# One block of p's projection made behind the gate blocks and kept, and the convolution's blocks summed on VectorE

## The chip, the cores and the metric

The kernel runs on one core of a Trainium2 chip. The metric is the device time of one execution in microseconds. TensorE multiplies matrices, VectorE does elementwise work with two operands, ScalarE does activations and copies, GpSimd (POOL) does small work and issues accumulating transfers, and SyncE (SP) issues the loads.

## The reference

One layer of a streaming encoder, for 512 tokens of width 1024, in float32:

```
h = h + 1/2 SwiGLU_1(RMSNorm(h))
z = RMSNorm(h) @ W_in                    # conv value | conv gate | q | k | v | r | low rank
y_conv = silu(LayerNorm(depthwise_conv31(a * sigmoid(b))))          # 512 channels
y_gla  = RMSNorm_per_head(chunked gated linear attention) * silu(r) # 4 heads of 128
h = h + concat([y_conv, y_gla]) @ W_out
h = h + 1/2 SwiGLU_2(RMSNorm(h))
h = h + sigmoid(RMSNorm(h) @ W_g) * (p @ W_p)                       # p: 512 x 256, W_p: 256 x 1024
out = RMSNorm(h)
```

## The kernel before, in words

**Products.** To keep float32 accuracy each operand is split into a rounded high part and a low part (the rest), and a product is three fast passes on TensorE: high by high, low by high, high by low. ScalarE makes the high part (a copy that rounds), VectorE the low part (a subtraction). For some weights the low part is made by ScalarE (times -1) and a transfer of GpSimd's queue that adds the original (`added`, L238). The mean of the LayerNorm is a product with a constant matrix `mean` in full float32, which TensorE runs as two slower passes.

**Layout.** Activations lie transposed: eight tiles `hT` of 128 channels by 512 tokens. The gate r and the values v are made per block of 128 tokens (`tokblock`, L1200). The convolution has four blocks of 128 channels, accumulators `acc[0]` to `acc[3]` (tiles named `cv` in the trace); each takes 31 steps ("taps") on VectorE, and `taps(n)` (L1016) puts n of them into VectorE's order at that place, alternating between two blocks. A step that finds its block finished issues nothing.

**Order.** `Ordered` (L36) fixes the order of TensorE, VectorE and ScalarE to the program's order through the whole stage that the change touches (`in_order(True)`, L996, to `in_order(False)`, L1801). GpSimd's and SyncE's instructions are issued by their own queues, in program order where they are ready.

**The stage of the change.** For t = 0 to 3 (L1365 to L1401) TensorE makes a gate block. Inside block 0 it also makes `outputs(0)` and inside block 1 `outputs(1)`, the attention's outputs, whose squares ScalarE sums at once. Behind block 1 VectorE runs `taps(15)`, then the root of the mean squares (`so`, `rso`; five taps between), ScalarE scales the sixteen head blocks (`y`), and VectorE multiplies each y by its silu(r). Then 16 transposes turn y into four banks `yps`; the products of `mean` with `acc[0]` and `acc[1]` stand before and behind the last four transposes. `gsplit` (L204) rounds each of the four turned heads (tiles `yg`). `first_part(n, ..)` (L1358) starts output block n with the four attention heads, 12 passes; blocks 0, 1, 4, 5, 2, 3 and 6 follow. VectorE meanwhile finishes the last convolution block, adds `acc[2]` and `acc[3]` into `acc23`, and the third mean product, in the middle of block 5, completes the LayerNorm's mean `mub`. From there VectorE, ScalarE and TensorE make the LayerNorm, whose results are the other four operands of the output product.

**The last stage.** p's transposed matrix is loaded behind the output weights (L1418) and split in the second FFN (`split_p`, at the units ("m2", 10) and ("m6", 10)). At the end `inputs(t, e)` (L1698) makes, for token block t and half e of the columns, p's product (`pq`, six passes) and turns h (`pt`, four transposes); `parts_of` (L1712) takes sigmoid, product, sum and squares. The last block but one is `inputs(0, 1)` (L1870).

**Buffers.** `bt` and `bt2` (L90 to L100) take halves of 20 buffers "A"; weights as loaded lie in six buffers "raw"; `bank()` (L127) goes round seven banks of PSUM, `aux()` has the eighth.

The places of the change, with their lines (the last stage of the gate blocks and the start of the output products):

```
1371        elif t == 1:
1372            ps = tokblock(wr, t, {2: lambda: outputs(1)})
1373            taps(15)
...
1402    yps = [bank() for _ in range(4)]
1403    mub = aux()
1404    for t in range(TB):
1405        if t == 3:
1406            pe.matmul(mub, mean, acc[0], start=True, stop=False)
1407        for h in range(4):
1408            pe.transpose(yps[h][:, t * P:(t + 1) * P], ytok[t][:, h * HV:(h + 1) * HV], ident)
1409    pe.matmul(mub, mean, acc[1], start=False, stop=False)
1410    taps(1)
1411    for h in range(4):
1412        mix[4 + h] = gsplit(yps[h], vec("gla_norm", h), "yg")
...
1436    first_part(5, wo[5], {6: lambda: pe.matmul(mub, mean, acc23, start=False, stop=True)})
```

Of the kernel before, what the change touches and what calls it, by code (L numbers as in the profile page):

```python
# [15 lines left out]
P = 128  # L16
# [46 lines left out]
def block_kernel(ctx: ExitStack, tc: tile.TileContext, a: dict, out: bass.AP):  # L63
# [38 lines left out]
    def cvt(dt=F32, s="cv"):  # L102
        return big.tile([P, SEQ], dt, tag="CV", bufs=NCV, name=nm(s))
# [134 lines left out]
    def added(w):  # L238

        h3, l3, r3 = w  # L240
        act.mul(l3, r3, -1.0)
        pool.dma_start(out=l3.bitcast(F32), in_=r3, accum_op=ALU.add)
        return w
# [754 lines left out]
    def pair(c0):  # L998

        return [load(w_in, 0, DC, c0 + i * P, P) for i in range(2)]  # L1000

    glu, acc, conv = [], [cvt() for _ in range(4)], []

    def conv_steps(c):
# [195 lines left out]
    def tokblock(w, t, mid={}):  # L1200

        ps = bank()
        ts = slice(t * P, (t + 1) * P)
        i = 0
        for k in range(DC):
            wh, wl = w[k // 2][:2]
            xh, xl = hg[k]
            for x, y in ((xh, wh), (xl, wh), (xh, wl)):
                if i in mid:
                    mid[i]()  # L1210
                pe.matmul(ps, x[:, ts], y[:, k % 2, :], start=(i == 0), stop=(i == 3 * DC - 1))
                i += 1
        return ps
# [64 lines left out]
    def outputs(t2):  # L1278
        ops.extend([bank(), bank()])
        for t in (2 * t2, 2 * t2 + 1):  # L1280
            for h in range(4):
                pe.matmul(out_of(t, h), sc[h][:, t, :], vt[t][:, h * HV:(h + 1) * HV],
                          start=(t % 2 == 0 and h < 2), stop=False, skip_group_check=True)
        for t in (2 * t2, 2 * t2 + 1):
            for j in range(2):
                for i in range(2):
                    c = 2 * t + i
                    for h in (2 * j, 2 * j + 1) if c else ():
                        d = slice((h % 2) * HK, (h % 2 + 1) * HK)
                        pe.matmul(out_of(t, h)[i * CH:(i + 1) * CH], qdec[j][d, c * CH:(c + 1) * CH],  # L1290
                                  states[j][c][0][d], start=False, stop=(t % 2 == j == 1), skip_group_check=True)
        for t in (2 * t2, 2 * t2 + 1):
            junk = tmp("sq", 2 * SEQ)[:, 0:SEQ]
            for h in range(4):
                act.activation(junk[:, h * HV:(h + 1) * HV], out_of(t, h), AF.Square,
                               accum_out=so[:, 4 * t + h:4 * t + h + 1])
# [7 lines left out]
    for t in range(TB):  # L1304
# [22 lines left out]
        if t == 0:  # L1327
            for j in range(2):
# [4 lines left out]
                act.copy(kd, kp)  # L1333
                kdt.append(kd)

    raw_o = {}

    def oload(n):
# [26 lines left out]
    for t in range(TB):  # L1365
        if t == 0:
            taps(3)
            ps = tokblock(wr, t, {5: lambda: chunk_sums([6]), 12: lambda: outputs(0)})
            chain(range(4, 7))
            oload(4)  # L1370
        elif t == 1:
            ps = tokblock(wr, t, {2: lambda: outputs(1)})
            taps(15)
            by_t = "p (t h) -> p t h"
            so3 = so.rearrange(by_t, h=4)
            dve.tensor_tensor(out=so3, in0=so3, in1=rs2.unsqueeze(2).to_broadcast([P, TB, 4]), op=ALU.mult)
            rso = rsqrt_mean(so, HV * HK, 16, between=lambda: taps(5))
            rso3 = rso.rearrange(by_t, h=4)
            dve.scalar_tensor_tensor(out=rso3, in0=rso3, scalar=HK ** -0.5,
                                     in1=rs.unsqueeze(2).to_broadcast([P, TB, 4]), op0=ALU.mult, op1=ALU.mult)  # L1380
        else:
            ps = tokblock(wr, t)
        r = bt(s="r")
        act.activation(r, ps, AF.Silu, scale=rs[:, t:t + 1])
        rt.append(r)
        if t == 1:
            oload(2)
            wo[4] = [added(w) for w in ohigh(4)]
            ytok = []
            for i in range(TB):  # L1390
                y = bt(s="y")
                for h in range(4):
                    vs = slice(h * HV, (h + 1) * HV)
                    act.activation(y[:, vs], out_of(i, h), AF.Copy, scale=rso[:, 4 * i + h:4 * i + h + 1])
                ytok.append(y)
        if t == 2:
            wo[5] = [added(w) for w in ohigh(5)]
        if t > 0:
            taps((0, 2, 5, 2)[t])
            for i in {1: (0,), 2: (1, 2), 3: (3,)}[t]:  # L1400
                dve.tensor_tensor(out=ytok[i], in0=ytok[i], in1=rt[i], op=ALU.mult)  # L1401
    yps = [bank() for _ in range(4)]
    mub = aux()
    for t in range(TB):
        if t == 3:
            pe.matmul(mub, mean, acc[0], start=True, stop=False)
        for h in range(4):
            pe.transpose(yps[h][:, t * P:(t + 1) * P], ytok[t][:, h * HV:(h + 1) * HV], ident)
    pe.matmul(mub, mean, acc[1], start=False, stop=False)
    taps(1)  # L1410
    for h in range(4):
        mix[4 + h] = gsplit(yps[h], vec("gla_norm", h), "yg")
    wo[2] = added(ohigh(2))
    wo[3] = ohigh(3)
    oload(6)


    p_raw = [bt(s="p") for _ in range(2)]  # L1418
    for k in range(2):
        nc.sync.dma_start(out=p_raw[k], in_=a["pT"][k * P:(k + 1) * P])  # L1420
    first_part(0, wo[0])
    first_part(1, wo[1])
    for steps in list(conv):
        for _ in steps:
            pass
    conv.clear()
    acc23 = bt(s="acc23")
    dve.tensor_tensor(out=acc23, in0=acc[2], in1=acc[3], op=ALU.add)
    low(wo[3])
    ffn2_in = a["ffn2_w_in"]  # L1430
    wf = {i: Left(ffn2_in, 2 * i) for i in range(3)}
# [1 line left out]
    w0.fetch("a11", "a12", "a21", "a22")  # L1433
    w1.fetch("a11", "a12")
    first_part(4, wo[4])
    first_part(5, wo[5], {6: lambda: pe.matmul(mub, mean, acc23, start=False, stop=True)})
    first_part(2, wo[2])
    sqs, lln, yc = [], [], []
    for c in range(4):
# [59 lines left out]
    for k in range(4):  # L1499
# [4 lines left out]
            pe.matmul(ps, wl, mix[k][0], start=False, stop=False)  # L1504
        for n in range(3):
            pe.matmul(half[n][1], rows_of(half[n][0], k)[0], mix[k][1], start=False, stop=(k == 3))
    pT = []

    def split_p(k):
        pT.append(split(p_raw[k], "pT"))  # L1510
# [54 lines left out]
    w1.part("s3")  # L1565
    w2.add_part("a12")
    hooks = sums_hooks(xb, ("t4",), (("m2", 1),))
    hooks.update({("m2", 10): lambda *_: split_p(0), ("m6", 10): lambda *_: split_p(1)})

    w_gate = a["ple_w_gate"]  # L1570
    q11, q21, q12, q22, b11, b21, t2, wproj = ([] for _ in range(8))
# [123 lines left out]
    sse = tmp("sse", 16, bufs=1)  # L1695
    hf, hl = {}, {}

    def inputs(t, e, small=False):  # L1698

        wh, wl = wproj[e][:2]  # L1700
        ts = slice(t * P, (t + 1) * P)
        pq, pt = bank(), aux() if small else bank()
        for k in range(2):
            xh, xl = pT[k]
            pe.matmul(pq, xh[:, ts], wh[:, k, :], start=(k == 0), stop=False)
            pe.matmul(pq, xl[:, ts], wh[:, k, :], start=False, stop=False)
            pe.matmul(pq, xh[:, ts], wl[:, k, :], start=False, stop=(k == 1))
        for c in range(4):
            pe.transpose(pt[:, c * P:(c + 1) * P], hT[4 * e + c][:, ts], ident)
        return pq, pt  # L1710

    def parts_of(t, e, z, pq, pt, c0=0, c1=SEQ, by=act):  # L1712
# [154 lines left out]
    i3 = inputs(3, 0, True)  # L1867
    z3 = plus(w_[1], both[:, 1])
    whole(2, 0, z2, *i2)
    i0 = inputs(0, 1)  # L1870
    times(x_, s4_, b22, last=True, blocks=((0,),))
    whole(3, 0, z3, *i3)
    cols = [slice(0, HALF), slice(HALF, SEQ)]
# [76 lines left out]
```

## Time and profile before

| | |
|---|---|
| median of 3 runs | 926.2 us (925.75 to 926.48) |
| profiled execution | 924.51 us, span 922.8 us |
| TensorE busy | 913.8 us (99%) |
| VectorE busy | 816.5 us (88%) |
| ScalarE busy | 509.3 us (55%) |
| mean granted clock of TensorE | 0.998 |

Times in the profile count from the start of the span. A row of a timeline gives start, duration, engine, line, operation, tiles (output <- inputs), shape and count, and in brackets how long the engine stood idle before it and which engine's instruction ended the wait. All instructions go through a helper, so their line is L46; they are told apart by their tiles. PEld are TensorE's weight loads, which overlap its products. The ends of matmuls are modelled, so the distance between two starts is the better measure of what one takes.

### The profile page before, as it was taken

The numbers are of one execution on the slowest core, as the hardware profiler recorded it, in microseconds if no ns is written. First come the engines' busy times: TensorE is split into PE (matmuls) and PEld (weight loads), VectorE is DVE, ScalarE is ACT, GpSimd is POOL, SyncE is SP. The second block draws the span as 40 slices with busy tenths as digits, with TensorE's granted clock in tenths as the row PEclk, the third lists the DMA queues.
The fourth block names the chain that finished last, engine by engine and source line by source line (L and its number), as shares of the span: only waits on it lengthen the run. The fifth ranks groups of instructions, "written<-read, shape, count | busy, mean of one in ns | idle before, by whom it ended". The sixth has DMA issues, their size and how long they took to land.

```text
span 922.8 us, 12837 instructions
## 1 busy us (share of the span) xinstructions
PE 913.8 (99%) x4952; PEld 780.3 (85%) x4952; DVE 816.5 (88%) x1091; ACT 509.3 (55%) x741; POOL 58.6 (6%) x75
## 2 busy tenths in 40 slices
PE   9999999999999999999999999999999999999996
PEld 8899888888888887788877889888888888888885
DVE  6699989999989776999996779899999999997996
ACT  7755354444454674463565875455445444456883
POOL 0120000000000111001120020000000000000121
PEclk9999999999999999999999999999999999999999
DMA  9534333223334692245562563333224322348463
GB/s 350 184 100 135 113 111 119 90 82 126 114 92 114 164 292 50 72 116 153 137 137 92 137 159 92 114 123 128 85 78 136 114 92 89 100 139 244 91 114 115
DMA packets 36317, 117.58 MB, mean 127 GB/s; under 512 B 4128, under 2 KB 4512, under 8 KB 36256
## 3 DMA queue, kind: packets, MB, share of 16 engines
q1 hardware_dynamic: 29776, 96.83, 31.7%
q0 software_dynamic: 6336, 19.93, 11.8%
q8 instruction: 39, 0.64, 0.3%
q14 instruction: 22, 0.18, 0.1%
q10 hardware_dynamic: 144, 0.00, 0.0%
HBM read 95.77 MB, written 2.10 MB: 106 GB/s over the span
## 4 chain that ended last, share of the span: by engine, by line
PE 99%; DVE 1%; issue 0%; ACT 0%; POOLq 0%; DVEq 0%
PE ps L46 59%; PE pd L46 40%; DVE u L46 0%; DVE rs L46 0%; ACT yc L46 0%; DVE y L46 0%; DVE g L46 0%; DVE s L46 0%; DVE lnsq L46 0%; POOLq L1946 0%; DVE ms L46 0%; DVE sse L46 0%; DVEq L46 0%; POOLq L46 0%
## 5 line engine op out<-in xcount | busy, mean ns | idle before, releaser
L46 DVE TENSOR_TENSOR wl<-wr,wh 128x1024 fp32r<-128x1024 f32 (+2 forms) x159 | 186.0, 1180 | 16.2 <-ACT wh L46 15.9
L46 ACT CAST wh<-wr 128x1024 fp32r<-128x1024 f32 (+2 forms) x177 | 175.3, 1022 | 15.9 <-PE ps L46 9.4
L46 PE MATMUL pd<-hg,wh 128*128 128x512 f32 x576 | 150.0, 391 | 0.0
L46 PE MATMUL ps<-act,wh 128*128 128x512 f32 x448 | 137.9, 389 | 0.0
L46 PEld LDWEIGHTS pd<-hg,wh 128*128 128x128 f32 x576 | 105.9, 188 | 21.1 <-DVE u L46 0.3
L46 PE MATMUL ps<-hg,wh 128*128 128x512 f32 (+1 forms) x448 | 117.0, 345 | 0.0
L46 PEld LDWEIGHTS ps<-act,wh 128*128 128x128 f32 x448 | 84.1, 188 | 17.5
L46 PE MATMUL pd<-t,wh 128*128 128x512 f32 x392 | 95.3, 391 | 0.0
L46 ACT ACTIVATE s<-g 128x512 f32<-128x512 f32 x48 | 30.4, 633 | 117.5 <-DVE g L46 117.5
L46 ACT COPY sq<-pd 128x1024 f32<-128x1024 f32 x45 | 45.8, 1017 | 86.7 <-PE pd L46 52.4
L46 PEld LDWEIGHTS ps<-hg,wh 128*128 128x128 f32 x448 | 78.1, 190 | 10.7 <-issue 0.6
L46 PE MATMUL ps<-act,wl 128*128 128x512 f32 x224 | 87.1, 389 | 0.0
L46 PEld LDWEIGHTS pd<-t,wh 128*128 128x128 f32 x392 | 71.4, 188 | 13.4
L46 PE MATMUL pd<-hg,wl 128*128 128x256 f32 (+1 forms) x544 | 81.5, 289 | 0.0
L46 PEld LDWEIGHTS pd<-hg,wl 128*128 128x128 f32 x544 | 73.9, 191 | 5.0
L46 PE MATMUL ps<-hg,wl 128*128 128x512 f32 (+1 forms) x224 | 77.0, 344 | 0.0
L46 ACT CAST wh<-sm 128x1024 fp32r<-128x1024 f32 x42 | 44.1, 1051 | 55.2 <-DVE sm L46 50.1
L46 DVE TENSOR_TENSOR wl<-sm,wh 128x1024 fp32r<-128x1024 f32 x42 | 51.1, 1220 | 4.9 <-ACT wh L46 4.9
L46 DVE TENSOR_TENSOR sq<-pd,sq 128x1024 f32<-128x1024 f32 x45 | 54.8, 1219 | 0.4 <-PE pd L46 0.4
L46 PE MATMUL ps<-wh,hg 128*128 128x512 f32 x176 | 54.7, 392 | 0.0
L46 PE MATMUL pd<-t,wl 128*128 128x256 f32 x392 | 52.4, 283 | 0.0
L46 PEld LDWEIGHTS pd<-t,wl 128*128 128x128 f32 x392 | 50.6, 191 | 1.5
(308 smaller groups left out, 1626.4 us busy)
## 6 DMA issues: line engine op xcount, KB each, us to landing
wr<-in_ffn_w_in SPq DMA_DIRECT2D x84, 512.0 KB, 3.6
wr<-in_ffn_w_out SPq DMA_DIRECT2D x32, 512.0 KB, 3.6
wl<-wr POOLq DMA_DIRECT2D x20, 512.0 KB, 5.4
wr<-in_ffn_w_out SPq DMA_DIRECT2D x16, 384.0 KB, 3.3
wr<-in_w_blocks SPq DMA_DIRECT2D x12, 512.0 KB, 4.9
wr<-in_w_rows SPq DMA_DIRECT2D x8, 512.0 KB, 3.8
wr<-in_w_out SPq DMA_DIRECT2D x8, 512.0 KB, 4.9
wq<-in_ple_w_gate SPq DMA_DIRECT2D x8, 512.0 KB, 4.3
```

The costliest lines, as they stand in the source:

```text
L46: inst = call(*args, **kwargs)
```

## The change

- `early_parts()` is new. It rounds the first 128 columns of p's transpose (`early_p`) on ScalarE, makes the low part on VectorE, and makes the parts of the second half of W_p's columns (`early_w`) by ScalarE and a transfer of GpSimd. It is called behind gate block 1, ahead of `taps(15)`. The two loads are issued ahead of the output weights.
- The six passes of p's product for token block 0 and column half 1 go into a bank `pq`: two ahead of the last four transposes of y, four behind them, in place of the first two mean products. ScalarE copies the bank to `kept_pq` behind the four `gsplit`. At the end `inputs(0, 1)` shrinks to the four transposes, and `parts_of` reads `kept_pq`.
- VectorE sums the convolution's blocks into `acc012`: `acc[0] + acc[1]` at t = 3, `acc[2]` behind the transposes, `acc[3]` at the end in place of `acc23`; the mean is one product, at the place of the third. `taps(2)` at t = 3 becomes `taps(1)`.
- Output block 0 is written out with its passes in another order: the high parts of a head are used before the low parts.
- The load of p moves from behind the output weights to the second FFN, unit ("m7", 9).

```diff
@@ -998,6 +998,14 @@
     def pair(c0):
 
         return [load(w_in, 0, DC, c0 + i * P, P) for i in range(2)]
+
+    def projected(pq, t, w, x, ks=range(2)):
+
+        ts = slice(t * P, (t + 1) * P)
+        for k in ks:
+            (xh, xl), (wh, wl) = x[k][:2], (v[:, k, :] for v in w)
+            for i, (y, v) in enumerate(((xh, wh), (xl, wh), (xh, wl))):
+                pe.matmul(pq, y[:, ts], v, start=(k == i == 0), stop=(k == 1 and i == 2))
 
     glu, acc, conv = [], [cvt() for _ in range(4)], []
 
@@ -1333,6 +1341,23 @@
                 act.copy(kd, kp)
                 kdt.append(kd)
 
+    early_w = raw(2, SEQ)
+    nc.sync.dma_start(out=early_w, in_=a["ple_w_proj"][0].rearrange("(k p) c -> p k c", p=P)[:, :, SEQ:])
+    early_p = tmp("u2", bufs=1)[:, 0:2 * P].rearrange("p (k c) -> p k c", k=2)
+    nc.sync.dma_start(out=early_p, in_=a["pT"].rearrange("(k p) c -> p k c", p=P)[:, :, 0:P])
+    kept_pq, kept_p = bt(s="pq"), bt(F32R, s="px")
+    early_x, early_wh = [], []
+
+    def early_parts():
+        hi, lo = (kept_p[:, i * 2 * P:(i + 1) * 2 * P].rearrange("p (k c) -> p k c", k=2) for i in range(2))
+        act.copy(hi, early_p)
+        dve.tensor_tensor(out=lo, in0=early_p, in1=hi.bitcast(F32), op=ALU.subtract)
+        early_x[:] = [(hi[:, k], lo[:, k]) for k in range(2)]
+        wh, wl = (wp.tile([P, 1024], F32R, tag="sm", bufs=2, name=nm("sm")).rearrange("p (k c) -> p k c", k=2)
+                  for _ in range(2))
+        act.copy(wh, early_w)
+        early_wh[:] = added((wh, wl, early_w))[:2]
+
     raw_o = {}
 
     def oload(n):
@@ -1370,6 +1395,7 @@
             oload(4)
         elif t == 1:
             ps = tokblock(wr, t, {2: lambda: outputs(1)})
+            early_parts()
             taps(15)
             by_t = "p (t h) -> p t h"
             so3 = so.rearrange(by_t, h=4)
@@ -1395,37 +1421,45 @@
                 ytok.append(y)
         if t == 2:
             wo[5] = [added(w) for w in ohigh(5)]
+        if t == 3:
+            acc012 = bt(s="acc012")
+            dve.tensor_tensor(out=acc012, in0=acc[0], in1=acc[1], op=ALU.add)
         if t > 0:
-            taps((0, 2, 5, 2)[t])
+            taps((0, 2, 5, 1)[t])
             for i in {1: (0,), 2: (1, 2), 3: (3,)}[t]:
                 dve.tensor_tensor(out=ytok[i], in0=ytok[i], in1=rt[i], op=ALU.mult)
     yps = [bank() for _ in range(4)]
-    mub = aux()
+    pq = bank()
     for t in range(TB):
         if t == 3:
-            pe.matmul(mub, mean, acc[0], start=True, stop=False)
+            for x in (0, 1):
+                pe.matmul(pq, early_x[0][x], early_wh[0][:, 0, :], start=(x == 0), stop=False)
         for h in range(4):
             pe.transpose(yps[h][:, t * P:(t + 1) * P], ytok[t][:, h * HV:(h + 1) * HV], ident)
-    pe.matmul(mub, mean, acc[1], start=False, stop=False)
+    pe.matmul(pq, early_x[0][0], early_wh[1][:, 0, :], start=False, stop=False)
+    projected(pq, 0, early_wh, early_x, (1,))
+    dve.tensor_tensor(out=acc012, in0=acc012, in1=acc[2], op=ALU.add)
     taps(1)
     for h in range(4):
         mix[4 + h] = gsplit(yps[h], vec("gla_norm", h), "yg")
+    act.copy(kept_pq, pq)
     wo[2] = added(ohigh(2))
     wo[3] = ohigh(3)
     oload(6)
 
 
-    p_raw = [bt(s="p") for _ in range(2)]
-    for k in range(2):
-        nc.sync.dma_start(out=p_raw[k], in_=a["pT"][k * P:(k + 1) * P])
-    first_part(0, wo[0])
+    ps = bank()
+    half[0] = (wo[0], ps)
+    todo = ((4, 0), (4, 1), (5, 0), (5, 1), (4, 2), (6, 0), (6, 1), (5, 2), (7, 0), (7, 1), (6, 2), (7, 2))
+    for n, (k, i) in enumerate(todo):
+        (wh, wl), (xh, xl) = rows_of(wo[0], k), mix[k]
+        pe.matmul(ps, (wh, wl, wh)[i], (xh, xh, xl)[i], start=(n == 0), stop=False)
     first_part(1, wo[1])
     for steps in list(conv):
         for _ in steps:
             pass
     conv.clear()
-    acc23 = bt(s="acc23")
-    dve.tensor_tensor(out=acc23, in0=acc[2], in1=acc[3], op=ALU.add)
+    dve.tensor_tensor(out=acc012, in0=acc012, in1=acc[3], op=ALU.add)
     low(wo[3])
     ffn2_in = a["ffn2_w_in"]
     wf = {i: Left(ffn2_in, 2 * i) for i in range(3)}
@@ -1433,7 +1467,8 @@
     w0.fetch("a11", "a12", "a21", "a22")
     w1.fetch("a11", "a12")
     first_part(4, wo[4])
-    first_part(5, wo[5], {6: lambda: pe.matmul(mub, mean, acc23, start=False, stop=True)})
+    mub = aux()
+    first_part(5, wo[5], {6: lambda: pe.matmul(mub, mean, acc012, start=True, stop=True)})
     first_part(2, wo[2])
     sqs, lln, yc = [], [], []
     for c in range(4):
@@ -1504,7 +1539,12 @@
             pe.matmul(ps, wl, mix[k][0], start=False, stop=False)
         for n in range(3):
             pe.matmul(half[n][1], rows_of(half[n][0], k)[0], mix[k][1], start=False, stop=(k == 3))
-    pT = []
+    pT, p_raw = [], []
+
+    def load_p():
+        for k in range(2):
+            p_raw.append(bt(s="p"))
+            nc.sync.dma_start(out=p_raw[k], in_=a["pT"][k * P:(k + 1) * P])
 
     def split_p(k):
         pT.append(split(p_raw[k], "pT"))
@@ -1565,7 +1605,7 @@
     w1.part("s3")
     w2.add_part("a12")
     hooks = sums_hooks(xb, ("t4",), (("m2", 1),))
-    hooks.update({("m2", 10): lambda *_: split_p(0), ("m6", 10): lambda *_: split_p(1)})
+    hooks.update({("m7", 9): lambda *_: load_p(), ("m2", 10): lambda *_: split_p(0), ("m6", 10): lambda *_: split_p(1)})
 
     w_gate = a["ple_w_gate"]
     q11, q21, q12, q22, b11, b21, t2, wproj = ([] for _ in range(8))
@@ -1695,18 +1735,15 @@
     sse = tmp("sse", 16, bufs=1)
     hf, hl = {}, {}
 
+    def turned(pt, t, e):
+        for c in range(4):
+            pe.transpose(pt[:, c * P:(c + 1) * P], hT[4 * e + c][:, t * P:(t + 1) * P], ident)
+
     def inputs(t, e, small=False):
 
-        wh, wl = wproj[e][:2]
-        ts = slice(t * P, (t + 1) * P)
         pq, pt = bank(), aux() if small else bank()
-        for k in range(2):
-            xh, xl = pT[k]
-            pe.matmul(pq, xh[:, ts], wh[:, k, :], start=(k == 0), stop=False)
-            pe.matmul(pq, xl[:, ts], wh[:, k, :], start=False, stop=False)
-            pe.matmul(pq, xh[:, ts], wl[:, k, :], start=False, stop=(k == 1))
-        for c in range(4):
-            pe.transpose(pt[:, c * P:(c + 1) * P], hT[4 * e + c][:, ts], ident)
+        projected(pq, t, wproj[e][:2], pT)
+        turned(pt, t, e)
         return pq, pt
 
     def parts_of(t, e, z, pq, pt, c0=0, c1=SEQ, by=act):
@@ -1867,7 +1904,9 @@
     i3 = inputs(3, 0, True)
     z3 = plus(w_[1], both[:, 1])
     whole(2, 0, z2, *i2)
-    i0 = inputs(0, 1)
+    pt0 = bank()
+    turned(pt0, 0, 1)
+    i0 = kept_pq, pt0
     times(x_, s4_, b22, last=True, blocks=((0,),))
     whole(3, 0, z3, *i3)
     cols = [slice(0, HALF), slice(HALF, SEQ)]
```

## The prediction

> **What bounds the kernel now.** I read the page first: the shares of busy time, then the chain that ended last.
>
> ```profile
> PE 913.8 (99%) x4952; PEld 780.3 (85%) x4952; DVE 816.5 (88%) x1091; ACT 509.3 (55%) x741; POOL 58.6 (6%) x75
> ...
> PE 99%; DVE 1%; issue 0%; ACT 0%; POOLq 0%; DVEq 0%
> ```
>
> TensorE has hardly a gap: time is won by taking work off it, and lost by any wait put in front of it. So I read next, engine by engine, the timeline of the stage that the change touches: the four gate blocks (to 471.3 us) and the output projection behind them. VectorE first:
>
> ```profile
> 448.82 1.38 DVE L46 SCALAR_TENSOR_TENSOR st<-st,decay,ps 128x128 f32<-128x128 f32 x5
> 450.11 0.73 DVE L46 SCALAR_TENSOR_TENSOR cv<-en,col,cv 128x488 f32<-128x488 f32 x1
> ...
> 459.81 0.18 DVE L46 TENSOR_TENSOR so<-so,rs 128x16 f32<-128x16 f32 x1
> ...
> 469.79 1.29 DVE L46 TENSOR_TENSOR y<-y,r 128x512 f32<-128x512 f32 x2
> ...
> 472.22 0.69 DVE L46 TENSOR_TENSOR y<-y,r 128x512 f32<-128x512 f32 x1 [0.50 <-ACT r L46]
> ```
>
> The states end at 450.1, `taps(15)` starts at once and ends at 459.8, and the means of the attention outputs (`so`) follow without a gap. VectorE is full here. ScalarE, in its own order:
>
> ```profile
> 457.41 0.25 ACT L46 ACTIVATION_READ_ACCUMULATOR sq<-ps 128x1 f32 x1
> 460.62 0.69 ACT L46 ACTIVATE r<-ps,rs 128x512 f32<-128x512 f32 x1 [2.96 <-PE ps L46]
> ...
> 464.71 4.24 ACT L46 ACTIVATE y<-ps,rs 128x128 f32<-128x128 f32 x16 [1.32 <-DVE rs L46]
> ...
> 471.50 0.69 ACT L46 ACTIVATE r<-ps,rs 128x512 f32<-128x512 f32 x1
> ```
>
> The squares of `outputs(1)` end at 457.66. The sixteen scalings `y` start when VectorE has their factors (464.71), and with the last gate `r` (471.50) ScalarE has run without a gap since then. So the last `y` product (472.22) is tied to VectorE's time at `so`. TensorE:
>
> ```profile
> 471.30 1.47 PE L46 MATMUL ps<-ident,y 128*128 128x128 f32 x12
> 472.61 1.02 PE L46 MATMUL ps<-cv,mean 128*128 128x512 f32 x2
> 473.47 0.60 PE L46 MATMUL ps<-ident,y 128*128 128x128 f32 x4
> 473.91 1.02 PE L46 MATMUL ps<-cv,mean 128*128 128x512 f32 x2
> 474.52 0.64 PE L46 MATMUL ps<-yg,wh 128*128 128x512 f32 x1
> ...
> 480.49 4.25 PE L46 MATMUL ps<-yg,wa 128*128 128x512 f32 x18
> 484.58 1.02 PE L46 MATMUL ps<-acc,mean 128*128 128x512 f32 x2
> ```
>
> The transposes of `y` follow the gate blocks with no slack worth naming: y of blocks 1 and 2 is ready at 471.08, the transposes begin at 471.30. The mean products stand where TensorE would wait for the last `y`.
>
> **The change part by part.** Times are those of the trace of before.
>
> *Mean products.* One takes 0.86 us of TensorE (472.61 to 473.47). Two go: -1.72.
>
> *The block of p's product.* Six wide products at 0.227 us each (18 in 484.58 - 480.49 = 4.09) come in here, +1.36, two ahead of the last four transposes and four behind them. The reordering of the first output block lets TensorE start on the rounded halves; between 474.52 + 0.25 (end of the mean) and 480.49, 24 products should take 5.45 and took 5.72, so about 0.3 us of waits for rounding goes. Taken alone, this stage would save about 0.5 us.
>
> *`early_parts()`: where the time is lost.* It stands behind gate block 1 and ahead of `taps(15)`. Its first instruction, ScalarE's copy of p's block, is queued behind the squares of `outputs(1)`, that is at 457.66. Its second is VectorE's subtraction, which needs that copy and in VectorE's program order stands where the taps now start, at 450.11. Both engines' orders are fixed by the kernel here, so VectorE stands from 450.11 with the fifteen taps, the `so` chain and everything else behind it. The nearest rows for the copies:
>
> ```profile
> L46 ACT CAST wh<-wr 128x1024 fp32r<-128x1024 f32 x159 | 161.5, 1046 | 15.9 <-PE ps L46 9.4 <-DVE wr L46 4.5 <-DMA wr<-in_first_w 1.7
> ...
> L46 ACT CAST hg<-xg 128x256 fp32r<-128x256 f32 x8 | 2.6, 404 | 0.0
> ```
>
> 457.66 + 0.40 = 458.06, and about 0.4 for the subtraction (a 512-wide product takes 0.69 at 472.22, so between half of it and all) gives 458.5; neighbours overlap by about 0.09 (448.82 + 1.38 against 450.11), so the taps start at 458.4: 8.3 us late. Bounds: 7.5 if the copy could start with the last square, 8.7 if it has a start cost like a hand-over. ScalarE's two further instructions (1.05 us each, the copies of 128x1024) fit in its idle 2.96 us before `r`; the accumulating transfer is issued by GpSimd near 460 and is past its queue before the power for `so`, which now comes at 468.5.
>
> Who waits: `so` moves from 459.81 to 468.1, the factors and the sixteen `y` from 464.71 to 473.0, the last `r` from 471.50 to 479.8, the last `y` product from 472.22 to 480.5, ending 481.2. TensorE ends the gate blocks at 471.3 as before (nothing there needs VectorE) and then stands, but for the transposes that come one block at a time.
>
> *To the mean.* Last transposes at 481.35 instead of 473.47; 0.45 for them, 0.91 for the four products, and 42 products (the blocks 0, 1, 4 and half of 5) at 0.227, 9.53: TensorE is at the mean at 492.25. VectorE:
>
> ```profile
> 474.50 2.73 DVE L46 SCALAR_TENSOR_TENSOR yg<-ps,col,yg 128x512 fp32r<-128x512 f32 x4 [0.94 <-ACT yg L46]
> 477.14 6.22 DVE L46 SCALAR_TENSOR_TENSOR cv<-en,col,cv 128x504 f32<-128x504 f32 x8
> 483.39 0.69 DVE L46 TENSOR_TENSOR acc<-cv,cv 128x512 f32<-128x512 f32 x1
> ```
>
> Its roundings start 1.03 behind the last transposes (474.50 - 473.47), so at 482.4, take 2.64, and then come nine taps instead of eight (`taps(2)` became `taps(1)`, and of the two steps before, one was the empty end of a finished block) at 0.78 each, 7.03, and the last sum, 0.69: 492.75. The first two sums fit where TensorE or VectorE waits: one stands in the tap's place before the 0.50 us wait for `r`, the other before the 0.94 us wait for `yg`. So TensorE waits another 0.5 us for the one mean product left and starts it at 492.8, 8.2 us later than 484.58. What follows (LayerNorm, rest of the projection, second FFN) hangs on this and is full again: all of it moves by 8.2.
>
> *The clock.* TensorE has never stood that long in this trace, except at its ends:
>
> ```profile
> 0.84 4.03 PE L46 MATMUL ps<-const-float32-0.0 128*128 128x128 f32 x18 [0.84 <-PEq L1940]
> ...
> 914.90:919.00 4.10, 0.00 (x0) 0.00 (x0) 3.26 (x15) 2.47 (x4) 0.54 (x1) 1.00 0.33 128
> 919.00:920.00 1.00, 0.00 (x0) 0.00 (x0) 0.06 (x1) 0.03 (x1) 0.00 (x0) 0.67 0.10 41
> ```
>
> The eighteen first passes take 0.22 us each where a 128-wide pass later takes 0.11 (twelve transposes in 1.31), for 4.0 us; and 4.4 us after TensorE has gone idle (no busy time from 914.9 on) the granted clock falls to half (0.67 over that slice is half from 919.34). In the changed kernel the stand is from 471.5 to 478.9 with 0.44 us of transposes at 475. I take it that the clock falls. Then 4.0 us from the last transposes on run at half rate and lose 2.0, of which 0.5 is hidden in the wait for the mean: +1.5. Bounds: 0 (the transposes keep it up) and 2.5 (the wake is later or nothing is hidden).
>
> [...]
>
> *The end.* The six products leave the last stage. There they are worth the same 1.36, but TensorE isn't alone:
>
> ```profile
> 910.22 0.67 ACT L46 ACTIVATE s<-ps,rs 128x512 f32<-128x512 f32 x1
> ```
>
> This sigmoid follows the scaling before it on ScalarE without a gap, so it can't move with TensorE, and on VectorE
>
> ```profile
> 913.09 0.42 DVE L46 TENSOR_TENSOR s<-s,ps 128x256 f32<-128x256 f32 x1 [0.68 <-PE ps L46]
> ...
> 915.61 0.41 DVE L46 TENSOR_TENSOR s<-s,ps 128x256 f32<-128x256 f32 x1
> ```
>
> only the 0.68 us wait at 913.09 can go; from there to the last block VectorE runs through. I take -0.7; bounds 0 and -1.36.
>
> *Costed at nothing.* The copy that keeps p's block is one more 128x512 pass of ScalarE, which falls in its idle time before the LayerNorm's squares, and costs 0.63 where that is gone:
>
> ```profile
> 486.36 0.63 ACT L46 ACTIVATE acc<-cv 128x512 f32<-128x512 f32 x1 [7.32 <-DVE cv L46]
> ```
>  The two early loads enter SP's queue ahead of eight loads of the output weights, which wait for buffers anyway and each get the next one; POOL's queue has one more transfer. p's own load moves to the second FFN, behind weight loads fetched seven units ahead: if it waits for a buffer it holds them, 0 to 2 us. The kept block holds a buffer to the end: 0 to 1.
>
> **Sum:** 8.2 + 1.5 - 0.7 = +9.0 on the profiled execution's 924.5 us (span 922.8), which lies 1.7 below the median of 926.2; so 935.2 for the median.
>
> **The rivals.**
> 1. *The clock stays up* because the transposes break the stand: 8.2 - 0.7 = +7.5, 933.7. For it: the only stand seen to halve the clock was unbroken for 4.4 us, and here the pieces are about 3.5 us.
> 2. *The subtraction doesn't hold VectorE* (no slowdown). One mechanism: p's copy runs before the squares. It decides if the copy is done by 450.1. Then the stage saves 0.5, but the sum of the four blocks ends at about 484.5, so the mean starts where it did, and only the end's 0.7 is left: 925.5, within 0.2%. Against: ScalarE's program order.
> 3. *A queue or buffer wait on top*: SP held by p's load, or a late buffer near the end: +2 on the forecast, 937.2.
>
> **How the numbers follow.** Forecast (stall and slow clock) 0.55, rival 1 0.27, rival 2 0.08, rival 3 0.08, rest 0.02 (faster). About 0.2% (1.9 us) is what a measurement of this kernel can tell from no change. Slower 0.90, same 0.08, faster 0.02. The range reaches from rival 1 less a spread of 1 us (bounds of copy and end) to rival 3: 932.6 to 937.3.
>
> **What would show it.** VectorE idle some 8 us near 450 to 458, released by ScalarE's 128x256 copy; the sixteen `y` at 473; TensorE idle in pieces between 471.5 and 481; the mean product at 493 to 495, released by VectorE; granted clock below 1 in the 5 us behind 478; the last stage shorter by less than 1.4. Wrong if VectorE's taps run through at 450.

## The result, and the profile after

The changed kernel takes 933.93 us (median of four runs, 933.12 to 934.93), the kernel before 925.98 beside it: a ratio of 1.0088, 95% interval 1.0076 to 1.0100. It is 8.0 us slower; 935.2 us were forecast. The profiled execution took 933.21 us with a span of 931.2; that of before took 924.51 with 922.8, so the two traces differ by 8.4 in span.

The page after, its line of busy times and the first line of its chain:

```profile
PE 914.9 (98%) x4948; PEld 781.1 (84%) x4948; DVE 818.5 (88%) x1094; ACT 512.1 (55%) x745; POOL 59.6 (6%) x76
...
PE 94%; issue 2%; DVE 2%; DMA 1%; POOL 1%; ACT 0%; POOLq 0%; DVEq 0%; ACTq 0%
```

TensorE has four instructions fewer and still carries the kernel, but its share of the chain falls from 99 to 94%: other engines now decide for some of the time. VectorE's timeline in the changed stage:

```profile
457.94 0.42 DVE L46 TENSOR_TENSOR px<-u,px 128x256 fp32r<-128x256 f32 x1 [7.79 <-ACT px L46]
458.28 0.72 DVE L46 SCALAR_TENSOR_TENSOR cv<-en,col,cv 128x488 f32<-128x488 f32 x1
...
467.98 0.17 DVE L46 TENSOR_TENSOR so<-so,rs 128x16 f32<-128x16 f32 x1
...
480.38 0.69 DVE L46 TENSOR_TENSOR y<-y,r 128x512 f32<-128x512 f32 x1 [0.54 <-ACT r L46]
...
485.12 7.00 DVE L46 SCALAR_TENSOR_TENSOR cv<-en,col,cv 128x503 f32<-128x503 f32 x9
492.15 0.69 DVE L46 TENSOR_TENSOR r<-r,cv 128x512 f32<-128x512 f32 x1
```

Here the time is lost. The subtraction (`px<-u,px`) stands 7.79 us and its releaser is ScalarE's copy; the first tap starts at 458.28 where it started at 450.11, the means `so` at 467.98 instead of 459.81, the last `y` product at 480.38 instead of 472.22: 8.17, 8.17 and 8.16 us late. ScalarE shows why the copy is late:

```profile
457.36 0.25 ACT L46 ACTIVATION_READ_ACCUMULATOR sq<-ps 128x1 f32 x1
457.45 0.45 ACT L46 CAST px<-u 128x256 fp32r<-128x256 f32 x1
...
472.88 1.14 ACT L46 ACTIVATE r<-ps,rs 128x128 f32<-128x128 f32 x4 [9.54 <-DVE rs L46]
```

The copy starts with the last square's result being read out, and ScalarE itself then waits 9.54 us for the `y` scalings (1.32 before; the first lands in a buffer that the trace calls `r`), for factors that VectorE makes late. TensorE, behind both:

```profile
474.90 0.64 PE L46 MATMUL ps<-ident,r 128*128 128x128 f32 x3 [3.49 <-ACT y L46]
476.91 0.48 PE L46 MATMUL ps<-ident,r 128*128 128x128 f32 x1 [1.37 <-ACT y L46]
478.69 1.97 PE L46 MATMUL ps<-ident,y 128*128 128x128 f32 x8 [1.30 <-DVE y L46]
...
488.67 4.24 PE L46 MATMUL ps<-yg,wa 128*128 128x512 f32 x18
492.90 1.12 PE L46 MATMUL ps<-r,mean 128*128 128x512 f32 x2
```

It stands 3.49, 1.37 and 1.30 us in front of the transposes and starts the mean at 492.90 (484.58 before, +8.32; the x2 are the two passes of the one mean product). Its weight load there shows what it waited for last:

```profile
492.90 0.30 PEld L46 LDWEIGHTS ps<-r,mean 128*128 128x128 f32 x2 [0.41 <-DVE r L46]
```

It was VectorE's last sum. In the last stage there is a wait that nothing in the forecast spoke of, TensorE's for a transfer that GpSimd issues (it adds the rounded-off rest of a weight block by DMA):

```profile
891.41 0.50 PE L46 MATMUL ps<-wl,s 128*128 128x512 f32 x1 [0.59 <-DMA wl<-wq]
```

And the end, VectorE's last block sums (before 913.09, with a wait of 0.68, and 915.61):

```profile
921.61 0.41 DVE L46 TENSOR_TENSOR s<-s,ps 128x256 f32<-128x256 f32 x1
...
924.14 0.41 DVE L46 TENSOR_TENSOR s<-s,ps 128x256 f32<-128x256 f32 x1
```

The 0.68 has gone; the last block is 8.53 late.

### The profile page after: what moved, and what is told of

The parts are those of the page before. It is cut to its first block, busy times and chain, and to the rows that moved or that the text cites. A ratio compares the mean times of both kernels' runs of the same rounds, so it can differ in the third digit from the quotient of the medians.

```text
span 931.2 us, 12847 instructions
## 1 busy us (share of the span) xinstructions
PE 914.9 (98%) x4948; PEld 781.1 (84%) x4948; DVE 818.5 (88%) x1094; ACT 512.1 (55%) x745; POOL 59.6 (6%) x76
## 4 chain that ended last, share of the span: by engine, by line
PE 94%; issue 2%; DVE 2%; DMA 1%; POOL 1%; ACT 0%; POOLq 0%; DVEq 0%; ACTq 0%
PE ps L46 55%; PE pd L46 40%; DMA wl<-wq 1%; POOL rs L46 0%; DVE cv L46 0%; DVE rs L46 0%; DVE y L46 0%; DVE s L46 0%; ACT wa L46 0%; POOL wa L46 0%; DVE g L46 0%; DVE u L46 0%; ACT yc L46 0%; ACT y L46 0%; DVE yc L46 0%
```

## The experiments

The theory: VectorE's subtraction, put in program order ahead of fifteen taps and behind a copy that ScalarE can make only after other work, holds VectorE for 7.8 us, and everything else is small. The rival: the added products, buffers and queue entries cost the time, and the wait only takes over idle time. The experiments ran in three groups (`e1_late_low` to `e4_keep_busy`, `e5_spin_aux` to `e8_before_order`, `e9_changed_again` to `e12_late_low_again`), each on one chip and beside its own runs of the kernel before. Times are medians; ratios are to the kernel before of the same group, with 95% intervals. Between groups only the ratios are compared, or the traces. Code is shown in part; `...` marks what is left out.

**1. The subtraction moved, nothing else** (`e1_late_low`, and again as `e12_late_low_again` beside the changed kernel).

```diff
...
     def early_parts():
...
         act.copy(hi, early_p)
-        dve.tensor_tensor(out=lo, in0=early_p, in1=hi.bitcast(F32), op=ALU.subtract)
+        early_lo[:] = [lambda: dve.tensor_tensor(out=lo, in0=early_p, in1=hi.bitcast(F32), op=ALU.subtract)]
...
         if t == 3:
             dve.tensor_tensor(out=acc012, in0=acc[0], in1=acc[1], op=ALU.add)
+            early_lo[0]()
```

> The changed kernel with one move: VectorE's 128x256 subtraction for p's block leaves its place ahead of taps(15) and stands at t == 3, behind the sum of acc0 and acc1. All the work of the change stays. Theory (the subtraction holds VectorE behind ScalarE's late copy, and everything after it slides): the taps start near 450 us instead of 458.3, the LayerNorm's mean starts at 484.6 +- 0.5 instead of 492.90, TensorE's clock stays at 1.00 through 474 to 484, and the total is 0.7 us below the kernel before (the tail's gain), or up to 1 us above that if the wait for a transfer at 891 us stays: 925.2 to 926.3 us. Rival (the lengthening is the cost of the added products, buffers or queue order, and the wait at the subtraction only takes over idle time that would come later): the mean still starts past 490 and the total stays above 931 us.

Measured: 925.21 us against 925.51, ratio 1.000 (0.999 to 1.001). The whole slowdown is gone. VectorE, and TensorE at the mean and in the last stage:

```profile
450.13 0.72 DVE L46 SCALAR_TENSOR_TENSOR cv<-en,col,cv 128x488 f32<-128x488 f32 x1
...
471.61 0.41 DVE L46 TENSOR_TENSOR px<-u,px 128x256 fp32r<-128x256 f32 x1
```

```profile
484.53 1.12 PE L46 MATMUL ps<-r,mean 128*128 128x512 f32 x2 [0.30 <-DVE r L46]
...
883.12 0.50 PE L46 MATMUL ps<-wl,s 128*128 128x512 f32 x1 [0.75 <-DMA wl<-wq]
```

The same subtraction costs no wait at 471.61; the mean starts where it did before (484.58). The wait for the transfer is still there, so it does not come from the stall. Repeated in one group with the changed kernel:

> The changed kernel itself, unaltered, beside the three below on the same chip, since its four runs and those of e5_spin_aux stood beside different runs of the kernel before. 7.8 to 8.4 us over the kernel before, some 933.3 to 934.

> The kernel of e1_late_low again, beside the changed kernel on the same chip: the price of the subtraction's place, taken directly. Theory: 8.3 to 8.9 us under e9_changed_again, 0 to 0.7 us under the kernel before. Rival (part of the first experiment's gain came from another place): 7.5 us or less.

Measured: changed kernel 934.1 (ratio 1.0089, 1.0075 to 1.0103), with the subtraction moved 925.13 (ratio 0.9996, 0.9987 to 1.0005). The place of one 0.42 us instruction is worth 9.0 us, a little over the expected 8.3 to 8.9; the rival of 7.5 or less falls.

**2. A smaller dose of the same wait** (`e2_early_copy`). ScalarE's copy moves ahead of the squares of `outputs(1)`, the subtraction stays.

```diff
...
     def early_parts():
...
-        act.copy(hi, early_p)
         dve.tensor_tensor(out=lo, in0=early_p, in1=hi.bitcast(F32), op=ALU.subtract)
...
         elif t == 1:
+            act.copy(hi, early_p)
             ps = tokblock(wr, t, {2: lambda: outputs(1)})
             early_parts()
```

> The changed kernel with only ScalarE's 128x256 copy of p's block moved ahead, to behind r[0], in front of the squares of the outputs that held it up; the subtraction keeps its place ahead of taps(15). A smaller dose of the same wait. Theory (VectorE stands from 450.1 until the copy has ended): the copy ends near 453.7, the wait is 3.6 us instead of 7.8, the mean starts at 488.2 +- 0.7, the clock stays at 1.00 or drops for less than 2 us, and the total lies 3 to 4.5 us over the kernel before (929 to 930.5). Rival (the place of VectorE's wait does not matter, the added work does): no change from the changed kernel, 933 to 934.5 us.

Measured: 929.92 (ratio 1.0051, 1.0035 to 1.0067), 4.4 over the kernel before. VectorE:

```profile
454.47 0.43 DVE L46 TENSOR_TENSOR px<-u,px 128x256 fp32r<-128x256 f32 x1 [3.45 <-ACT px L46]
454.81 0.72 DVE L46 SCALAR_TENSOR_TENSOR cv<-en,col,cv 128x488 f32<-128x488 f32 x1
```

The taps are 4.7 us late (454.81 against 450.11) and the total is up by 4.4; in the changed kernel they are 8.2 late and the total is up by 8.0 to 8.4. The time follows the dose, roughly: the profiled execution is the slowest of the four (930.43, the others up to 929.95). TensorE's mean,

```profile
489.82 1.12 PE L46 MATMUL ps<-r,mean 128*128 128x512 f32 x2 [0.31 <-DVE r L46]
```

came 0.9 later than the end of the band I gave (488.2 with 0.7 on either side). I had put the copy's end at 453.7; VectorE could go on only at 454.5 and reached the taps at 454.8, 4.7 late instead of 3.6. And a second wait was added, for GpSimd's root of the mean squares:

```profile
468.98 0.18 DVE L46 TENSOR_TENSOR rs<-rs 128x16 f32<-128x16 f32 x1 [0.84 <-POOL rs L46]
```

In the kernel before this wait is 0.21.

**3. The wait alone, put into the kernel before** (`e3_wait_alone`; the loaded block, its copy and the difference are not used by anything).

```diff
...
             ps = tokblock(wr, t, {2: lambda: outputs(1)})
...
+            act.copy(hi, early_p)
+            dve.tensor_tensor(out=lo, in0=early_p, in1=hi.bitcast(F32), op=ALU.subtract)
             taps(15)
```

> The kernel before with the wait alone: the early load of p's block, ScalarE's 128x256 copy and VectorE's subtraction are put ahead of taps(15) as in the changed kernel, their result is not used, and nothing else of the change is made: the mean keeps its three products, p's product is made where it was. Theory (the wait is the whole cost): VectorE is idle for 7.8 us at the subtraction, the mean over acc2 + acc3 comes 8 to 8.7 us later, and the total is 8 to 9.3 us over the kernel before: 934 to 935.3 us, that is 0.7 us over the changed kernel, since the tail's gain is absent. Rival (the wait is harmless by itself): within 1 us of the kernel before.

Measured: 934.89 (ratio 1.0102, 1.0086 to 1.0118), 9.4 over the kernel before, 0.1 above the band. One copy and one subtraction in the wrong place make the old kernel as slow as the changed one:

```profile
457.90 0.42 DVE L46 TENSOR_TENSOR px<-u,px 128x256 fp32r<-128x256 f32 x1 [7.79 <-ACT px L46]
```

**4. The clock.** The forecast priced TensorE's slower clock at 1.5 us. To keep it up, extra products fill the gaps in which TensorE stood.

```diff
     for t in range(TB):
+        for _ in range(14 if t < 2 else 0):
+            pe.matmul(pq, early_x[0][0], early_wh[0][:, 0, :], start=True, stop=True)
         if t == 3:
```

> The changed kernel with 14 more 128x512 products into the bank of p's product, half of them ahead of the transposes of block 0 and half of them ahead of those of block 1, written over by the real product later: TensorE has work where it stood idle, about 3.3 us for each seven at full clock or 6.6 for fourteen ahead of either block. Theory (the halved clock at 476 to 482 us costs nothing, because TensorE waits for VectorE's sum at the mean anyway): the clock reads 1.00 throughout 470 to 490, the mean still starts at 492.9 +- 0.3 and the total is that of the changed kernel within 0.4 us. Rival (the halved clock is on the path and costs 1.5 us, as forecast): the total falls by 1 to 2 us, to 932 to 933 us.

This run (`e4_keep_busy`) has 14 products ahead of each of the two blocks, so 28 where its expectation speaks of 14 (and at 0.227 us each seven products take 1.6 us, not the 3.3 it gives). It missed: 939.16 us (1.0153, 1.0137 to 1.0169). The products write the bank of p's product, and that bank was not free:

```profile
477.41 6.17 PE L46 MATMUL ps<-sm,px 128*128 128x512 f32 x14 [5.77 <-ACT y L46]
483.42 0.60 PE L46 MATMUL ps<-ident,r 128*128 128x128 f32 x4
483.78 3.45 PE L46 MATMUL ps<-sm,px 128*128 128x512 f32 x14
```

They waited for ScalarE's reading of `y`, as the transposes did, ran largely at half rate and pushed the rest back. It says nothing on the clock's price. The next one (`e5_spin_aux`) writes a bank that nothing uses then; its extra products are used by nothing:

```diff
-    pq = bank()
+    pq, spin = bank(), aux()
     for t in range(TB):
+        for _ in range((14, 5, 4, 0)[t]):
+            pe.matmul(spin, early_x[0][0], early_wh[0][:, 0, :], start=True, stop=True)
```

> The changed kernel with 23 more 128x512 products of p's block into a PSUM bank that nothing else uses at that time (14 ahead of the transposes of block 0, 5 ahead of block 1, 4 ahead of block 2; their result is not used), so that TensorE has work in the gaps of 3.49, 1.37 and 1.30 us in which it stood. At 0.23 us each they fill 3.2, 1.1 and 0.9 us. Theory (the halved clock at 476 to 482 us costs nothing at the mean, since TensorE still waits 0.41 us there for VectorE's last sum): the clock reads 1.00 throughout 470 to 490, the mean still starts at 492.9 +- 0.3, TensorE's wait for the sum grows, and the total is that of the changed kernel within 0.5 us: 933.4 to 934.4. Rival (the halved clock is on the path and costs 1.5 us, as forecast): 932 to 932.8 us.

Measured: 932.3 us (ratio 1.0076, 1.0064 to 1.0089), the rival's band, 1.6 below the changed kernel's first median. But the two medians stand beside different runs of the kernel before (925.3 and 925.98), and the trace gives the rival less. TensorE with the extra products:

```profile
471.04 3.33 PE L46 MATMUL ps<-sm,px 128*128 128x512 f32 x14
...
492.47 1.13 PE L46 MATMUL ps<-r,mean 128*128 128x512 f32 x2 [0.34 <-DVE r L46]
```

The mean comes 0.43 earlier than in the changed kernel, and VectorE's first tap was already 0.20 earlier in that execution (458.08 against 458.28), so the clock's price at the mean is 0.2 in this pair of traces. The rest of this trace's gain comes later: the wait for the transfer (0.59 after) does not occur in it. Two causes were mixed, so both had to be varied on one chip. The last stage's order (next experiment) takes the transfer's wait away; with it, once without and once with the extra products:

> The changed kernel with the last stage's ScalarE order of e6_late_low_order. Theory (its wait of 0.59 us, and 1.01 at the weight load, for the late transfer at 891 us is real and the order takes it away): 0.8 to 1.2 us under e9_changed_again. Rival (that wait was one execution's accident): within 0.3 us of it.

> The kernel of e5_spin_aux with the same ScalarE order, to price the halved clock without the late transfer beside it: against e10_changed_order only the 23 extra products differ. Theory (most of the clock's loss lies inside the wait for VectorE's sum, and what is left is the 0.2 us by which the slow transposes delay VectorE's scalings): 0.2 to 0.5 us faster than e10_changed_order. Rival (the full price forecast): 1.2 to 1.6 us faster.

Measured: the changed kernel 934.1, with the order (`e10_changed_order`) 933.11, with order and products (`e11_spin_order`) 932.2. So the order is worth 1.0, as the transfer's theory said, and the extra products 0.9, between the 0.2 to 0.5 and the 1.2 to 1.6. Both steps are small for this measurement: the intervals of `e9_changed_again` (1.0075 to 1.0103), `e10_changed_order` (1.0067 to 1.0092) and `e11_spin_order` (1.0060 to 1.0085) overlap, each with the next. The traces bear out the first step (experiment 5). What the clock did in each profiled execution shows in the windows 470 to 490 us (after the window and its length stand the busy times of PE, PEld, DVE, ACT and POOL, then the granted clock, the DMA share and GB/s). First the changed kernel:

```profile
470.00:490.00 20.00, 13.84 (x59) 11.01 (x58) 18.74 (x33) 13.21 (x30) 4.48 (x4) 0.83 0.42 98
```

The changed kernel again (`e9_changed_again`):

```profile
470.00:490.00 20.00, 14.10 (x56) 11.07 (x55) 18.77 (x33) 13.21 (x30) 5.06 (x4) 0.74 0.37 92
```

With the order (`e10_changed_order`):

```profile
470.00:490.00 20.00, 13.85 (x58) 10.93 (x57) 18.77 (x32) 13.20 (x30) 4.73 (x4) 0.83 0.39 95
```

With order and products (`e11_spin_order`):

```profile
470.00:490.00 20.00, 18.32 (x81) 14.51 (x80) 18.16 (x32) 13.20 (x30) 5.18 (x4) 0.91 0.35 87
```

With the products alone (`e5_spin_aux`):

```profile
470.00:490.00 20.00, 18.04 (x85) 13.83 (x84) 18.87 (x33) 13.23 (x30) 4.28 (x4) 1.00 0.43 102
```

In the changed kernel's trace the clock reads 0.50 throughout 476 to 482. A mean of 0.83 over 20 us is 6.8 us at half rate, 0.74 is 10.4, 0.91 is 3.6. What this costs up to the mean shows in the time from the first tap to the mean:

| execution | granted clock, 470 to 490 | first tap to mean | us |
|---|---|---|---|
| changed kernel | 0.83 | 458.28 to 492.90 | 34.62 |
| `e9_changed_again` | 0.74 | 458.87 to 493.89 | 35.02 |
| `e10_changed_order` | 0.83 | 458.54 to 493.39 | 34.85 |
| `e11_spin_order` | 0.91 | 459.00 to 494.26 | 35.26 |
| `e5_spin_aux` | 1.00 | 458.08 to 492.47 | 34.39 |

The kernel before, `e1_late_low`, `e12_late_low_again`, `e6_late_low_order`, `e7_tail_made_again` and `e8_before_order`, all at 1.00, take 34.40 to 34.47. In `e10_changed_order` VectorE's last sum had ended at 493.09 (492.40 + 0.69) and TensorE came to the mean later, without a wait, so there the slow stretch before it was on the path:

```profile
493.39 1.02 PE L46 MATMUL ps<-r,mean 128*128 128x512 f32 x2
```

So the slow clock costs 0.2 to 0.6 at the mean in three executions of the changed kernel without extra products (against `e5_spin_aux`), depending on where the slow time falls. In `e11_spin_order` the clock fell in spite of the products, for half as long, and the products themselves, at half rate, then stood in the way (the five from 477.72 took 2.48 us, 1.41 in `e5_spin_aux`); its profiled execution is the slowest of its five (933.66, the others 932.12 to 932.41). So the price stays open between 0.2 (trace) and 0.9 (medians); the 1.5 of the forecast is outside.

**5. The late transfer, and the tail.** In the last stage ScalarE is held to cast, negate, cast, negate:

```diff
+    act.on, act.last = True, None
     b3 = [added(later_high(t)) for t in t3]
+    act.on = False
```

> The kernel with VectorE's late subtraction (the first experiment), and one more edit in the last stage: ScalarE is held to cast, negate, cast, negate for the two weight blocks of which GpSimd then adds the rest by DMA, where it went cast, cast, negate, negate. The first of the two transfers can then be issued 0.95 us earlier (near 876.2 instead of 877.12). Theory (the 0.75 us that TensorE waits at 883.1 us for this transfer ate the tail's gain): the wait goes and the total falls by 0.5 to 0.9 us against the first experiment, to 924.3 to 924.7, 0.8 to 1.2 us below the kernel before. Rival (the two transfers share the DMA engines, so that an earlier start gains little, or another wait follows): within 0.3 us of the first experiment, 924.9 to 925.5.

Measured, on the kernel with the subtraction moved (`e6_late_low_order`): 923.85 us against 925.3, ratio 0.9983 (0.9974 to 0.9992). This version is 1.5 us below the kernel before, and 0.45 below the band that its theory gave. GpSimd's issues of the two transfers in the timeline, first in the kernel before:

```profile
877.02 0.86 POOL L46 DMA_DIRECT2D wl<-wq  x1 [14.44 <-ACT wl L46]
878.11 0.86 POOL L46 DMA_DIRECT2D wl<-wq  x1 [0.23 <-DVE s L46]
```

In the changed kernel:

```profile
885.60 1.75 POOL L46 DMA_DIRECT2D wl<-wq  x2 [14.46 <-ACT wl L46]
```

With the new order (`e6_late_low_order`):

```profile
876.53 0.86 POOL L46 DMA_DIRECT2D wl<-wq  x1 [13.51 <-ACT wl L46]
878.28 0.86 POOL L46 DMA_DIRECT2D wl<-wq  x1 [0.89 <-DVE n L46]
```

Before, the second issue stood 0.23 us for a VectorE result, and the two were 1.09 us apart; after, they follow each other at once, and the first lands 5.8 us after its issue instead of 4.6. With the new order they are 1.75 apart and TensorE doesn't wait in any of the five profiled executions that have it. The first landed 5.8 to 6.3 us after its issue, with a wait on TensorE, in five executions with issues at once (changed kernel twice, `e1_late_low`, `e2_early_copy`, `e12_late_low_again`), but without a wait in two others (`e4_keep_busy`, `e5_spin_aux`): it is an event that comes often, not always, and what decides it is open. Why the second issue no longer waits for VectorE is open: the change gives other buffers to the last stage's tiles, and no run varied that alone. The control, the new order in the kernel before (`e8_before_order`):

> The kernel before with the ScalarE order of e6_late_low_order alone, as its control: what this edit is worth without the change. Theory: TensorE waits only 0.20 us for these transfers in the kernel before, so at most 0.2 us: 925.2 to 925.6. Rival (the transfers' times vary from execution to execution and the order is worth as much here): 0.5 to 0.9 us faster than before.

Measured: 924.82 (ratio 0.9995, 0.9986 to 1.0004), 0.5 below the kernel before and 1.0 above `e6_late_low_order`. That is below the theory's band and at the edge of the rival's; its interval holds 1, so medians don't settle it. The trace does for its own execution: from the mean to VectorE's last block sum it takes 431.01 us, the kernel before 431.03. The last run makes the tail's six products again (`e7_tail_made_again`; the kept copy is made and not used):

```diff
-    pt0 = bank()
-    turned(pt0, 0, 1)
-    i0 = kept_pq, pt0
+    i0 = inputs(0, 1)
```

> The kernel of e6_late_low_order with the last stage's p product of block 0 made again by its six products, as in the kernel before; the kept copy is still made and not used. It prices the tail's part of the change by itself. Theory (VectorE's waits bound the end, so the six products' 1.37 us are worth 0.7): 0.5 to 0.9 us slower than e6_late_low_order, the last block of VectorE 0.7 us later. Rivals: TensorE bounds the end (1.2 to 1.4 us slower), or the products are hidden there (within 0.2 us).

Measured: 924.82 (ratio 0.9997, 0.9988 to 1.0006), 0.97 above `e6_late_low_order`, a little over the theory's 0.5 to 0.9 and below the 1.2 of the rival. VectorE's next-to-last block in the timeline of `e7_tail_made_again`:

```profile
913.69 0.42 DVE L46 TENSOR_TENSOR s<-s,ps 128x256 f32<-128x256 f32 x1 [0.69 <-PE ps L46]
```

And of `e6_late_low_order`:

```profile
912.70 0.41 DVE L46 TENSOR_TENSOR s<-s,ps 128x256 f32<-128x256 f32 x1
```

The wait of 0.69 us is back with the products. Of the 0.99 between the two rows 0.27 stood between the executions already at the first tap (450.69 against 450.42), which leaves 0.72. This is the tail's price, and it bears out that VectorE, not TensorE (1.37), bounds it.

The time from the mean's start to VectorE's last block sum puts the tail and the transfer side by side, free of what happened before the mean:

| executions | us |
|---|---|
| six products in the tail (kernel before, `e3_wait_alone`, `e7_tail_made_again`, `e8_before_order`) | 430.99 to 431.10 |
| tail without them, no wait for the transfer (`e4_keep_busy`, `e5_spin_aux`, `e6_late_low_order`, `e10_changed_order`, `e11_spin_order`) | 430.29 to 430.42 |
| tail without them, with the wait (changed kernel twice, `e1_late_low`, `e2_early_copy`, `e12_late_low_again`) | 431.24 to 431.74 |

So the shorter tail saves 0.6 to 0.8 in every execution, and the wait, where it comes, takes 0.8 to 1.5.

## Why the prediction was right, and where it wasn't

*The stall* (8.3 us at the taps, 8.2 at the mean) was right to 0.15: 8.17 at the taps, 8.32 at the mean, of which some 0.2 is the clock. The bounds of 7.5 and 8.7 came from whether ScalarE's copy overlaps the last square; it starts 0.16 before the read-out ends (457.45 against 457.36 + 0.25), a little toward the lower end. Each link showed: the copy behind the squares, VectorE with its taps behind the copy, the `y` behind VectorE, TensorE idle in pieces, the mean released by VectorE's last sum with 0.41 us of wait (0.5 forecast). That the wait is the cause, and not the rest of the change, is shown from three sides: taken away (`e1_late_low`), halved (`e2_early_copy`), and put alone into the old kernel (`e3_wait_alone`).

*The clock* did fall, but its term of 1.5 was too large; rival 1, in which it stays up, gave 933.7, nearer to the median of 933.9 than the forecast, and yet its mechanism did not happen: that nearness is luck. The step that failed is "4.0 us from the last transposes on run at half rate". I started the slow stretch at 481.35. In the trace TensorE is at work again from 478.69, with the transposes of blocks 1 and 2, and the clock is back near 482.5 (0.50 in 480 to 482, 0.88 in 482 to 484). Most of the slow time thus lay where TensorE had to wait for the last `y` in any case (its product ends at 481.07); only some 1.4 us of it lay on TensorE's path, a loss of 0.7, and 0.41 us of wait at the mean was still left. Measured: 0.2 to 0.6 at the mean in single executions, 0.9 by the medians.

*A term that was missing* made up for it: the transfer that comes late at 891 us, 1.0 us by the medians of `e9_changed_again` and `e10_changed_order`, 0.8 to 1.5 by the traces. The forecast had priced queue and buffer waits at nothing, with 0 to 2 us as a rival and with other mechanisms (SP held by p's load, a late buffer). It is of that kind but not of that place: a wait on GpSimd that had spread two transfers is gone, and the first then often lands late.

*The end* (-0.7, bounds 0 and -1.36): -0.72 by `e7_tail_made_again`. It was right, with its mechanism.

*The mean products and the block of p's product* ("taken alone, this stage would save about 0.5", but the mean then waits for the four-block sum): with the subtraction moved the mean starts at 484.53 against 484.58, released by VectorE. That part saves nothing, as rival 2 had it. (Its terms, -1.72, +1.36 and -0.3, add up to 0.7 rather than 0.5; it makes no difference here.)

In sum 8.3 (mean) + 1.0 (transfer) - 0.7 (end) = 8.6, beside 8.4 in the spans and 8.0 to 8.4 in the medians. The forecast's total was nearer than its terms, by luck: one too large by about 1 and one missing of about 1.

## What to carry to other kernels

Before an instruction goes into a full engine's program order, look up what its producer is queued behind on the *other* engine; the price is that engine's whole lag, not the instruction's time (here 8 us for 0.42). When a stage stalls, work out from where TensorE resumes, however thin its work, before a slow clock is priced, and then how much of that stretch it would have waited in anyway. When a good change shows no gain, look for a second wait far away: here the repaired change alone was level with the old kernel, and 1.5 us faster once a transfer two stages later was issued earlier.

## What the runs showed of the hardware

In the windows 470 to 490 us (twice what the mean clock lacks to 1.00, times 20 us) the time at half rate was 6.8 us in the changed kernel, in `e10_changed_order`, in `e3_wait_alone` and in `e4_keep_busy` (0.83 each), 10.4 in `e9_changed_again` (0.74), 3.6 in `e11_spin_order` (0.91) and none in `e5_spin_aux` (1.00). In the changed kernel's trace slices of 2 us read 0.91 in 474 to 476, 0.50 in the three up to 482 and 0.88 in 482 to 484, which adds up to 6.84. Why one and the same kernel had 6.8 once and 10.4 the other time, and why the clock fell in `e11_spin_order` and not in `e5_spin_aux`, the same program up to the last stage, no run shows. The 4.0 us of slow time that the forecast took from the trace of before is passed in five of these executions; the loss of 2.0 drawn from it did not come, since most of the slow time lay in waits.

I had not expected the fall to need so little idle time. In `e9_changed_again` TensorE stopped at 472.00, and its first three transposes, from 475.48, took 0.89 us, against 0.65 in `e5_spin_aux` at a clock of 1.00: it was slow after a stand of 3.48. In `e10_changed_order` it stopped at 471.67, and after as long a stand, 3.48, the same three took 0.64 from 475.15; the fourth, at 477.16, took 0.47 (0.33 in `e5_spin_aux`). In the changed kernel it stopped at 471.41 and the clock fell near 475.6. In `e2_early_copy`, where TensorE stood 1.37 and 1.44 us in pieces from 472.7 to 475.8, it didn't fall at all (1.00 over 470 to 490).
